# Two attention branches of a decoder trunk: row maxima formed negated, one denominator sum per four blocks, and a new ratio in which the branches are interleaved

## The chip, the cores and the metric

One Trainium2 chip; the kernel runs as one program on one of its cores. The metric is device time in microseconds (us) of one execution. The profile is one execution of the program taken by the hardware profiler; the unprofiled runs are timed on their own.

## What is computed

A decoder layer over 2048 tokens of width 1024: a normalised and modulated input, one wide projection, two attention branches, their merge through gates and an output projection, then a SwiGLU feed-forward part and a last norm. What matters here is the two attention branches and their merge, all in float32:

```python
# branch A: 12 heads in three groups of (window, dilation); per head and 128-query block
logits = where(valid, q.k * Dh**-0.5 - slope * distance, -inf)
lse = logsumexp(logits); out = softmax(logits) @ v
# the three groups of a head slot are merged with weights softmax(lse over the groups)
ya = sum_g alpha_g * out_g @ w_up_a
# branch B: 4 heads, causal, with a forgetting bias
s = q.k * Dh**-0.5 + (F[t] - F[s]);  yb = softmax(where(s_pos <= t_pos, s, -inf)) @ v @ w_up_b
merged = sigmoid(gza) * ya + sigmoid(gzb) * yb
```

## The kernel before, in words

The program goes through stages: modulation and first projection with its gates (to about 880 us in the profile), the two attention branches, the up-projection with the gates (`up`), the output projection with the residual (`p3_block`), and the feed-forward part. Large products are written as Strassen-like products (`t_blocks`) of operands split in a high and a low part (`split`, L106 on ACT and L107 on DVE), and three matmuls stand for one (`mm3`, L100 to L102).

**Branch A** (`head_a`): for each of 12 heads and four groups `u` of four 128-query blocks, `scores` runs two matmuls a block into PSUM tile X (L754, L758), adds the bias and takes the row maximum in one DVE instruction (`tensor_tensor_reduce`, L760; the profile shows a second, short one that reads out the accumulator). When all four blocks are done L763 forms the negative of the four maxima (`nm`), and ACT takes the exponential (L768). `sums` transposes the result on PE (L785), copies it out (L792), multiplies with the values (L796) and lets ACT copy the sum to `utok` (L808). At a head's end its maxima are transposed (L814) and stored in `sta`.

**Branch B** (`head_f`): for each of 4 heads and 16 query blocks (8 pairs `cq`), `scores` goes over 512-key segments: POOL forms the bias `bi` (L838, and L843 on the diagonal), PE the scores (L850), DVE the sum with the running maximum `mx` (L852), then the negative of the last one (L858, `nmf`), ACT the exponentials with their sums `dp` (L862), and DVE adds the segment sums of the block to one denominator (L864). `sums` takes, after every second pair, the reciprocal of four denominators (L869), transposes them (L871) and stores them (`rc`), and for every pair transposes the exponentials (L886), splits them (L106, L107, tiles `ph` and `pl`) and multiplies with the values (L894).

**The merge** (`merge_load`, `merge_weights`): from the stored maxima and denominators of the three groups come the weights `mw`, which go to DRAM as `wrow` (L970). `up` loads the branch outputs `uw` (L981) and the weights spread over the partitions (L987), multiplies and adds them on POOL or DVE (L989, L991), splits them to `y`, and for eight column blocks loads a weight panel (L1001) and gates `gt` (L1008), runs 12 matmuls into PSUM tile Z for each half (L100 to L102, `psZ<-y,wu`), multiplies by the gate on DVE (L1014) and adds on POOL (L1015).

**The order of the work.** `branch_a` and `branch_b` are generators that yield a cost after each step; `together` advances the one whose clock is lower, with A's cost multiplied by `PACE[0]`. A's steps sum to 12 x 4 x 3.5 = 168, B's to 167.2 (per head 136 x 0.175 for the scores and 18 for the sums). A's factor of 0.6 therefore puts its end at 100.8 on B's clock, six tenths of the way through B. After that B goes on alone until it is half way through its last head (`f_done >= 14`), then `up(0)` is interleaved with the rest of it, and `up(1)` follows. A scheduler then moves the instructions of each engine by its own estimate of their times; each engine, and each queue that issues transfers, takes its instructions strictly in the order that comes out. All transfers here are issued by SP's queue. Tiles come from slots with a fixed number of buffers: `wh` and `wl` hold B's exponentials and later gates of `up(1)`, `pc` A's exponentials and later gates of `up(0)`, `bigx` A's `utok` and later `uw`.

```python
    ga, gb = branch_a(), branch_b()
    together([(ga, PACE[0]), (gb, 1.0)])
    merge_weights()
    together([(gb, 1.0)], lambda: f_done[0] >= 4 * (NHB - 1) + 2)
    gu = up(0)
    together([(gu, PACE[1]), (gb, 1.0)])
    for g in (gb, gu, up(1)):
        for _ in g: pass
```

## Time and profile before

| what | value |
|---|---|
| median of three runs | 2900.26 us (2892.75 to 2901.07) |
| the profiled execution's own time | 2897.54 us |
| its span, first to last instruction | 2895.8 us |
| PE, DVE, ACT, POOL busy | 96%, 70%, 48%, 7% of the span |
| mean granted TensorE clock | 0.988 |

PE is TensorE's matmuls, PEld its weight loads, DVE VectorE, ACT ScalarE, POOL GpSimd, SP the engine whose queue issues the transfers. A busy share is that of the whole span; the stages differ, so the rows further down are taken by stretch. A wait is put down to what ended it. [...]

### The profile page before, as it was taken

How to read it: one execution, taken by the hardware profiler on the slowest of the kernel's cores; microseconds unless marked ns; L12 is line 12 of the kernel's file. 1: busy time of each engine (PE TensorE's matmuls, PEld its weight loads, DVE VectorE, ACT ScalarE, POOL GpSimd, SP SyncE). 2: the span in 40 equal slices, each digit the busy share in tenths (PEclk: the TensorE clock that was granted, in tenths of full speed). 3: DMA queues.
4: the chain of work that ended last, by engine and by line, in shares of the span. 5: the costliest groups of instructions: out<-in, count | busy, mean ns of one | idle time of the engine just before them, and what ended most of it. 6: DMA issues, size and time to landing. Idle time of an engine off the chain costs nothing.

```text
span 2895.8 us, 40840 instructions
## 1 busy us (share of the span) xinstructions
PE 2774.1 (96%) x13778; PEld 2309.5 (80%) x13778; DVE 2041.0 (70%) x4269; ACT 1376.4 (48%) x2726; POOL 213.9 (7%) x305
## 2 busy tenths in 40 slices
PE   7999999999999999888899999999999999989998
PEld 6789888978887878666677788888888888868876
DVE  5865578576646887687967766657755558795987
ACT  4654335344447777653356533335333335343543
POOL 0000000000002222563200000000000000000000
PEclk9999999999999999998999999999999999999999
DMA  7687466467757668569766554444522235785642
GB/s 242 166 226 220 131 207 204 148 168 212 235 176 261 239 176 259 144 176 310 265 211 207 189 178 138 135 146 137 164 86 79 83 109 179 217 264 168 219 155 99
DMA packets 520858, 530.52 MB, mean 183 GB/s; under 512 B 91556, under 2 KB 372540, under 8 KB 514236
## 3 DMA queue, kind: packets, MB, share of 16 engines
q1 hardware_dynamic: 520648, 527.91, 58.6%
q8 instruction: 108, 1.77, 0.3%
q14 instruction: 102, 0.84, 0.1%
HBM read 356.51 MB, written 171.29 MB: 182 GB/s over the span
## 4 chain that ended last, share of the span: by engine, by line
PE 47%; DVE 3%; ACT 1%; DMA 1%; issue 1%; DVEq 0%; ACTq 0%
PE psX L100 9%; PE psX L101 9%; PE psX L102 9%; PE psZ L100 4%; PE psZ L101 4%; PE psZ L102 4%; PE psY L101 2%; PE psY L102 2%; PE psY L100 2%; DVE wl L107 0%; DVE wt L217 0%; PE psT L1090 0%; ACT wh L106 0%; ACT u L244 0%; DMA wr<-act 0%
## 5 line engine op out<-in xcount | busy, mean ns | idle before, releaser
L106 ACT ACTIVATE wh<-wt 128x512 fp32r<-128x512 f32 (+1 forms) x464 | 288.5, 623 | 637.0 <-PE psX L101 344.6
L107 DVE TENSOR_TENSOR wl<-wt,wh 128x512 fp32r<-128x512 f32 (+1 forms) x464 | 314.6, 681 | 257.8 <-ACT wh L106 240.6
L106 ACT ACTIVATE wh<-wr 128x512 fp32r<-128x512 f32 (+1 forms) x324 | 201.5, 623 | 433.1 <-PE psX L101 239.1
L107 DVE TENSOR_TENSOR wl<-wr,wh 128x512 fp32r<-128x512 f32 (+1 forms) x324 | 220.0, 680 | 200.9 <-ACT wh L106 183.2
L217 DVE TENSOR_TENSOR wt<-wr 128x512 f32<-128x512 f32 (+1 forms) x216 | 146.5, 678 | 12.0 <-DMA wr<-in_w_in_dram 5.1
L217 DVE TENSOR_TENSOR wt<-wr,wt 128x512 f32<-128x512 f32 (+1 forms) x216 | 147.8, 684 | 3.8
L244 ACT ACTIVATE u<-psX 128x512 f32<-128x512 f32 x216 | 125.3, 580 | 8.1 <-PE psX L102 8.1
L838 POOL TENSOR_SCALAR bi<-nf,F_col 128x512 f32<-128x512 f32 (+3 forms) x160 | 104.9, 658 | 229.3 <-DVE mx L852 192.3
L862 ACT ACTIVATE L<-L,nmf 128x512 f32<-128x512 f32 (+3 forms) x160 | 103.1, 647 | 20.7 <-DVE nmf L858 20.5
L894 PE MATMUL psY<-ph,vhl 128*128 128x256 f32 (+1 forms) x288 | 82.4, 299 | 9.1 <-ACT ph L106 7.8
L1120 DVE TENSOR_TENSOR ac<-psZ,u 128x512 f32<-128x512 f32 x88 | 60.4, 687 | 42.2 <-PE psZ L102 41.2
L894 PE MATMUL psY<-pl,vhl 128*128 128x256 f32 (+1 forms) x288 | 81.8, 312 | 7.8 <-DVE pl L107 6.8
L106 ACT ACTIVATE ph<-psT 128x512 fp32r<-128x512 f32 (+1 forms) x101 | 56.2, 568 | 53.5 <-PE psT L886 53.3
L796 PE MATMUL psY<-pf,va 128*65 128x128 f32 (+1 forms) x408 | 77.7, 324 | 1.3 <-DVE pf L792 0.9
L760 DVE CUSTOM_DVE_ANT_0 L<-psX,bias 128x128 f32<-128x128 f32 (+1 forms) x192 | 64.6, 357 | 19.8 <-PE psX L758 14.1
L107 DVE TENSOR_TENSOR pl<-psT,ph 128x512 fp32r<-128x512 f32 (+1 forms) x101 | 64.5, 646 | 16.2 <-ACT ph L106 16.0
L768 ACT ACTIVATE L<-L,nm 128x128 f32<-128x128 f32 (+1 forms) x192 | 72.1, 450 | 5.5 <-DVE nm L763 4.5
L100 PE MATMUL psZ<-y,wu 128*128 128x512 f32 x128 | 55.7, 435 | 18.7 <-DVE gt L1014 11.5
L100 PE MATMUL psX<-f_A11h,wh 128*128 128x512 f32 x176 | 69.4, 394 | 0.0
L894 PEld LDWEIGHTS psY<-ph,vhl 128*128 128x128 f32 x288 | 56.7, 197 | 15.6 <-ACT ph L106 10.9
L102 PE MATMUL psX<-f_A11h,wl 128*128 128x512 f32 x176 | 69.1, 393 | 0.0
L101 PE MATMUL psX<-f_A11l,wh 128*128 128x512 f32 x176 | 69.1, 392 | 0.0
(536 smaller groups left out, 8732.6 us busy)
## 6 DMA issues: line engine op xcount, KB each, us to landing
x<-x SPq DMA_DIRECT2D x192, 256.0 KB
wr<-in_w_ffn_in_dram SPq DMA_DIRECT2D x88, 512.0 KB
wr<-in_w_in_dram SPq DMA_DIRECT2D x64, 512.0 KB
qk<-sh SPq DMA_DIRECT2D x192, 128.0 KB
act<-ac SPq DMA_DIRECT2D x88, 256.0 KB
pc<-wfg SPq DMA_DIRECT2D x77, 256.0 KB
qk<-st SPq DMA_DIRECT2D x128, 128.0 KB
wa<-in_w_ada_dram SPq DMA_DIRECT2D x64, 256.0 KB
```

The costliest lines, as they stand in the source:

```text
L100: PE.matmul(o, lh, rh, start=first, stop=False, skip_group_check=True)
L101: PE.matmul(o, lh, rl, start=False, stop=False, skip_group_check=True)
L102: PE.matmul(o, ll, rh, start=False, stop=last, skip_group_check=True)
L106: A.activation(hi, src, AF.Copy)
L107: V.tensor_tensor(lo, src, raw(hi), op=ALU.subtract)
L217: V.tensor_tensor(v[i], *made[i](g, v), op=ALU.subtract)
L244: A.activation(t, o, AF.Copy, scale=1.0 if scale is None else scale)
L768: A.activation(Lb(b, o0, 256), Lb(b, o0, 256), AF.Exp, bias=nm[:, bb:bb + 1])
L796: PE.matmul(uo[:65, qb_[0] * P:qb_[0] * P + w], va[:, 4 * u + kb_, :], pf[:, pos:pos + w], start=i_ == 0, stop=i_ == len(runs) - 1, skip_g ...
L838: G.tensor_scalar(bi[:, :e - sg], nf[sg // D][:, sg % D:sg % D + e - sg], 1.0, F_col[:, qb * NHB + h:qb * NHB + h + 1], op0=ALU.mult, op1= ...
L862: A.activation(Ls[cq, b, sg][:, :e - sg], Ls[cq, b, sg][:, :e - sg], AF.Exp, bias=nm, accum_out=dp[:, i:i + 1])
L894: PE.matmul(uo[:, q0:256], vhl[:, kb, :], p_[:, 256 * i:256 * i + 256 - q0], start=(kp == 0 and i == 0 and j == 0), stop=(last and i == 1 ...
```

## The change

A `tensor_tensor_reduce` with scale -1 and a minimum in place of a maximum writes the negated score and accumulates the negated row maximum; the exponential is taken with scale -1. So L763 (48 instructions) and L858 (64) are gone, and A's exponential of a block needs that block's reduction alone. The merge takes a minimum of negated maxima and turns one subtraction round. B's segment sums of four blocks lie in one tile and are added by one instruction just before the reciprocal: 16 in place of 64. `PACE[0]` goes from 0.6 to 0.82, which puts A's end at 168 x 0.82 = 137.8 on B's clock; B's last head is half through at 136.7. A filler tile grows from 16 to 32 columns. In the changed kernel the lines are a few lower: L753 and L755 are A's scores, L765 its exponential, L793 its product with the values, L811 its last transpose, L836 and L841 B's bias, L848 its scores, L857 its exponential, L881 and L889 its transposes and products, L965 `wrow`, L976 and L982 `uw`, L984 and L986 the products of the merge, L996 the panel, L1003 the gates, L1010 POOL's addition.

```diff
-PACE = (0.6, 0.6)
+PACE = (0.82, 0.6)
...
-    cst.tile([P, 16], F32, name="fill")
+    cst.tile([P, 32], F32, name="fill")
     ident = cst.tile([P, P], F32, name="ident")
...
         G.tensor_scalar(bias, base, float(slopes[h] * d), 0.0, op0=ALU.mult, op1=ALU.add)
-        mx = sm.tile([P, NT], F32, tag="mxa", name="mxa")
         nm = sm.tile([P, NT], F32, tag="nm", name="nm")
...
                 V.tensor_tensor_reduce(out=Lb(b, o0, 256), in0=so[:, o0:], in1=bias[:, o0:],
-                                       scale=1.0, scalar=NEG, op0=ALU.add, op1=ALU.max,
-                                       accum_out=mx[:, bb:bb + 1])
-            V.tensor_scalar(nm[:, 4 * u:4 * u + 4], mx[:, 4 * u:4 * u + 4], -1.0, None,
-                            op0=ALU.mult)
+                                       scale=-1.0, scalar=-NEG, op0=ALU.add, op1=ALU.min,
+                                       accum_out=nm[:, bb:bb + 1])
             for b in range(4):
...
                 o0 = P if first[b] else 0
-                A.activation(Lb(b, o0, 256), Lb(b, o0, 256), AF.Exp, bias=nm[:, bb:bb + 1])
+                A.activation(Lb(b, o0, 256), Lb(b, o0, 256), AF.Exp, bias=nm[:, bb:bb + 1], scale=-1.0)
             return Lb, first
...
             pst = ps("Y")
-            PE.transpose(pst[:NT, :P], mx, ident)
+            PE.transpose(pst[:NT, :P], nm, ident)
             str_ = slot("pc", "str", [NT, P])
...
             if cq % 2 == 0 and b == 0:
-                den[cq // 2] = sm.tile([P, 4], F32, tag="den", name="den", bufs=4)
+                den[cq // 2] = [sm.tile([P, 4, cq // 2 + 1], F32, tag=f"dp{cq // 2}", name="dp"),
+                                sm.tile([P, 4], F32, tag="den", name="den")]
             qb = 2 * cq + b
             nk = (qb + 1) * P
-            dq = den[cq // 2][:, qb % 4:qb % 4 + 1]
-            mx = sm.tile([P, 4], F32, tag="mx", name="mx", bufs=4)
+            dp = den[cq // 2][0][:, qb % 4, :]
+            nm = sm.tile([P, 4], F32, tag="nmf", name="nmf", bufs=4)
             segs = list(range(0, nk, CH))
...
                     out=L[:, :e - sg], in0=s[:, :e - sg], in1=bi[:, :e - sg],
-                    scale=1.0, scalar=NEG if i == 0 else mx[:, i - 1:i],
-                    op0=ALU.add, op1=ALU.max, accum_out=mx[:, i:i + 1])
+                    scale=-1.0, scalar=-NEG if i == 0 else nm[:, i - 1:i],
+                    op0=ALU.add, op1=ALU.min, accum_out=nm[:, i:i + 1])
             n = len(segs)
-            nm = sm.tile([P, 1], F32, tag="nmf", name="nmf", bufs=4)
-            V.tensor_scalar(nm, mx[:, n - 1:n], -1.0, None, op0=ALU.mult)
-            dp = sm.tile([P, 4], F32, tag="dp", name="dp", bufs=4)
             for i, sg in enumerate(segs):
                 e = min(sg + CH, nk)
-                A.activation(Ls[cq, b, sg][:, :e - sg], Ls[cq, b, sg][:, :e - sg], AF.Exp, bias=nm,
-                             accum_out=dp[:, i:i + 1])
-            V.tensor_reduce(out=dq, in_=dp[:, :n], op=ALU.add, axis=mybir.AxisListType.X)
+                A.activation(Ls[cq, b, sg][:, :e - sg], Ls[cq, b, sg][:, :e - sg], AF.Exp,
+                             bias=nm[:, n - 1:n], scale=-1.0, accum_out=dp[:, i:i + 1])
...
             if cq % 2:
-                dn = den[cq // 2]
+                dp, dn = den[cq // 2]
+                V.tensor_reduce(out=dn, in_=dp, op=ALU.add, axis=mybir.AxisListType.X)
                 V.reciprocal(dn, dn)
...
         for g in (1, 2):
-            V.tensor_tensor(v3(M, g), v3(M, g), tok(g), op=ALU.max)
+            V.tensor_tensor(v3(M, g), v3(M, g), tok(g), op=ALU.min)
         for g in range(3):
-            V.tensor_tensor(v3(es[g], g), tok(g), v3(M, g), op=ALU.subtract)
+            V.tensor_tensor(v3(es[g], g), v3(M, g), tok(g), op=ALU.subtract)
             A.activation(es[g], es[g], AF.Exp)
```

Three places show what the change does to the order of the instructions. Rows are those of one engine, in its order; a number behind x says how many like it follow each other.

**PE, where branch A ends.** The matmuls of the two branches and of `up` stand between the first score matmul (number 0) and the last of `up` (number 2,813 in both programs). Before, A's last instruction is number 1,815, the first row here, and what follows is B alone (scores L850, transposes L886, products L894):

```order
L814 MATMUL psY<-ident,mxa 16x128
L886 MATMUL psT<-ident,L 128x128 x4
L894 MATMUL psY<-ph,vhl 128x256
L871 MATMUL psY<-ident,den 4x128
L850 MATMUL psX<-kh,qs 128x512
L850 MATMUL psX<-kl,qs 128x512
L894 MATMUL psY<-pl,vhl 128x256
L894 MATMUL psY<-ph,vhl 128x256
L894 MATMUL psY<-pl,vhl 128x256
```

Of the change, numbers 1,826 to 1,837:

```order
L753 MATMUL psX<-kl,qs 128x128
L889 MATMUL psY<-ph,vhl 128x256
L753 MATMUL psX<-kh,qs 128x128
L753 MATMUL psX<-kl,qs 128x128
L753 MATMUL psX<-kh,qs 128x128
L753 MATMUL psX<-kl,qs 128x128
L889 MATMUL psY<-pl,vhl 128x256
L889 MATMUL psY<-ph,vhl 128x256
L889 MATMUL psY<-pl,vhl 128x256
L889 MATMUL psY<-ph,vhl 128x256
L848 MATMUL psZ<-kh,qs 128x512
L848 MATMUL psZ<-kl,qs 128x512
```

A's scores (L753) stand here between B's. A's last instruction is number 2,154, so 339 instructions of B have moved ahead of A's end; the first matmul of `up` is number 2,315 (before 2,158), and B's last one number 2,427 (before 2,547).

**POOL and SP, at the merge.** POOL forms B's bias and, in the same queue, multiplies the branch outputs with the merge weights (`uw`). Before, from the last rows ahead of the first such product on:

```order
L838 TENSOR_SCALAR bi<-nf,F_col 128x512
L843 AFFINE_SELECT bi<-bi 128x128
L989 TENSOR_TENSOR uw<-uw 128x1024
L838 TENSOR_SCALAR bi<-nf,F_col 128x512 x2
L838 TENSOR_SCALAR bi<-nf,F_col 128x384
L989 TENSOR_TENSOR uw<-uw 128x1024
L991 TENSOR_TENSOR uw<-uw 128x1024
L838 TENSOR_SCALAR bi<-nf,F_col 128x512
L843 AFFINE_SELECT bi<-bi 128x128
```

and B's bias goes on like this: 47 bias instructions and 18 diagonals stand behind the first product. Of the change, to the point from which there is no bias any more:

```order
L841 AFFINE_SELECT bi<-bi 128x128
L836 TENSOR_SCALAR bi<-nf,F_col 128x512
L984 TENSOR_TENSOR uw<-uw 128x1024
L836 TENSOR_SCALAR bi<-nf,F_col 128x512
L984 TENSOR_TENSOR uw<-uw 128x1024
L986 TENSOR_TENSOR uw<-uw 128x1024
L836 TENSOR_SCALAR bi<-nf,F_col 128x512 x2
L986 TENSOR_TENSOR uw<-uw 128x1024
L841 AFFINE_SELECT bi<-bi 128x128
L984 TENSOR_TENSOR uw<-uw 128x1024
```

Here three bias instructions and one diagonal are left behind the first product. SP's queue takes gates and panels of `up` ahead of the weights now. Before, the rows up to the weights (`wrow`) are:

```order
L811 DMA u_200<-utok 64x2048
L812 DMA den<-utok 1x2048
L943 DMA md<-sta 32x16x4
L874 DMA rc<-dro 4x128
L936 DMA md<-den 128x64
L981 DMA uw<-u_199 128x1024
L970 DMA wrow<-mw 128x64 x3
L987 DMA uw<-wrow 64x1024 x6
```

and of the change:

```order
L901 DMA u_202<-uy 64x512
L1003 DMA gt<-g_0_163 128x512
L1003 DMA gt<-g_1_132 128x512
L1003 DMA gt<-g_1_164 128x512
L996 DMA wr<-in_w_up_a_dram 128x2x128
L996 DMA wr<-in_w_up_b_dram 128x2x128
L869 DMA rc<-dro 4x128
L1003 DMA gt<-g_0_135 128x512
L1003 DMA gt<-g_0_167 128x512
L965 DMA wrow<-mw 128x64 x3
L1003 DMA gt<-g_1_136 128x512
L982 DMA uw<-wrow 64x1024 x6
```

Four weight panel transfers and seven gate transfers stand ahead of the spread weights (two of the panels and the first gate a few rows further up), where before the first panel stood 27 transfers behind `wrow`.

**ACT, where the exponentials begin.** The last gates of the projection stage take a sigmoid (L445, L448), and going over to an exponential takes a table load. Before:

```order
L862 ACT_TABLE_LOAD
L862 ACTIVATE L,dp<-L,nmf 128x128
L445 ACT_TABLE_LOAD
L445 ACTIVATE st<-psX 128x512
L448 ACTIVATE st<-st 128x512
L768 ACT_TABLE_LOAD
L768 ACTIVATE L<-L,nm 128x128
L768 ACTIVATE L<-L,nm 128x256 x3
L862 ACTIVATE L,dp<-L,nmf 128x256
L862 ACTIVATE L,dp<-L,nmf 128x384
L448 ACT_TABLE_LOAD
```

and of the change:

```order
L765 ACT_TABLE_LOAD
L765 ACTIVATE L<-L,nm 128x128
L448 ACT_TABLE_LOAD
L448 ACTIVATE st<-st 128x512 x2
L765 ACT_TABLE_LOAD
L765 ACTIVATE L<-L,nm 128x256
L244 ACTIVATE u_8666<-psX 128x512
L765 ACTIVATE L<-L,nm 128x256
L857 ACTIVATE L,dp<-L,nmf 128x128
L445 ACT_TABLE_LOAD
L445 ACTIVATE st<-psX 128x512
L765 ACT_TABLE_LOAD
```

A's exponentials go one by one, between the sigmoids, and the table is loaded nine times before it stays, in place of five; in the whole program there are 14 loads in place of 10.

## Rows read from the trace of the kernel before

**Rows 1.** The page's first two parts: the span with busy time, share and instruction count of PE and DVE, and the granted clock in 40 slices (tenths).

```profile
span 2895.8 us, 40840 instructions
...
PE 2774.1 (96%) x13778; PEld 2309.5 (80%) x13778; DVE 2041.0 (70%) x4269; ACT 1376.4 (48%) x2726; POOL 213.9 (7%) x305
...
PEclk9999999999999999998999999999999999999999
```

**Rows 2.** Busy time of the engines by stretch: both branches, B alone, `up`, the gap behind it, and the output projection. Columns: length, then busy us (and instructions) of PE, PEld, DVE, ACT and POOL, the granted clock, the DMA engines' busy share, GB/s.

```profile
880.00:1178.00 298.00, 282.80 (x1994) 244.47 (x1993) 240.69 (x942) 232.16 (x556) 82.36 (x164) 1.00 0.71 223
1178.00:1258.00 80.00, 61.39 (x351) 50.21 (x349) 59.32 (x170) 47.12 (x121) 50.24 (x58) 0.89 0.41 109
1258.00:1423.00 165.00, 143.20 (x674) 113.79 (x674) 134.11 (x230) 63.75 (x134) 73.11 (x58) 0.95 0.93 298
1423.00:1448.00 25.00, 18.33 (x62) 13.18 (x63) 25.00 (x41) 10.82 (x19) 1.58 (x1) 0.80 0.45 141
1448.00:1550.00 102.00, 100.20 (x469) 81.46 (x467) 73.25 (x173) 56.34 (x120) 0.00 (x0) 1.00 0.64 207
```

**Rows 3.** Where the stretches begin and end: A's last transpose and the matmuls of `up`, from the views of line 814 and of tile y (duration min/median/max in ns, first and last start in us).

```profile
L814 PE MATMUL psY<-ident,mxa x12: 271/272/277, 919.5 to 1178.5; 128*16 128x128 f32 x12
```

```profile
L100 PE MATMUL psZ<-y,wu x128: 388/395/797, 1257.8 to 1417.9; 128*128 128x512 f32 x128
L106 ACT ACTIVATE y<-uw x16: 612/626/632, 1212.6 to 1359.7; 128x512 fp32r<-128x512 f32 x16
```

**Rows 4.** PE's waits from 1178 to 1258 us: what waited for what, total us, times, longest.

```profile
PE psY L894 <- ACT ph L106: 5.2, 5, 2.1
PE psY L894 <- DVE pl L107: 3.5, 4, 2.4
PE psX L850 <- DVE mx L852: 3.4, 4, 1.8
PE psZ L850 <- DVE mx L852: 3.1, 3, 1.6
```

**Rows 5.** POOL in order of time behind A's end (start us, us, instruction, and in brackets the idle time before it and what ended it).

```profile
1187.18 0.29 POOL L843 TENSOR_SCALAR_AFFINE_SELECT bi<-bi 128x128 f32<-128x128 f32 x1
1196.70 2.40 POOL L989 TENSOR_TENSOR uw<-uw 128x1024 f32<-128x1024 f32 x1 [9.23 <-issue]
1199.07 2.94 POOL L838 TENSOR_SCALAR bi<-nf,F_col 128x512 f32<-128x512 f32 x3
1201.98 2.37 POOL L989 TENSOR_TENSOR uw<-uw 128x1024 f32<-128x1024 f32 x1
```

**Rows 6.** ACT in order of time in the same stretch, two rows.

```profile
1197.71 0.38 ACT L901 ACTIVATE ulf<-psY 64x256 f32<-64x256 f32 x1 [3.00 <-PE psY L894]
1201.72 0.72 ACT L862 ACTIVATE L<-L,nmf 128x512 f32<-128x512 f32 x1 [3.63 <-DVE nmf L858]
```

**Rows 7.** SP's queue in order of time at the merge (start us, us, line, transfer, count).

```profile
1184.90 0.34 SPq L936 DMA_DIRECT2D md<-den  x1
...
1190.36 1.27 SPq L970 DMA_DIRECT2D wrow<-mw  x3
1191.81 3.66 SPq L987 DMA_DIRECT2D uw<-wrow  x6
```

**Rows 8.** PE's and DVE's waits from 1258 to 1448 us, the longest.

```profile
PE psZ L100 <- DVE gt L1014: 11.5, 10, 4.6
PE psZ L100 <- ACT wu L106: 6.4, 2, 3.5
```

```profile
DVE gt L1014 <- PE psZ L102: 8.3, 10, 2.1
DVE wu L107 <- ACT wu L106: 6.1, 1, 6.1
```

**Rows 9.** Bytes moved from 1178 to 1258 us and from 1258 to 1423 us, one line of each answer of the transfer view.

```profile
DMA packets 4385, 8.76 MB, mean 109 GB/s; under 512 B 1597, under 2 KB 2137, under 8 KB 4313
```

```profile
DMA packets 35880, 49.23 MB, mean 298 GB/s; under 512 B 3006, under 2 KB 17866, under 8 KB 35867
```

**Rows 10.** The instructions that the change removes: groups by line on DVE from 875 to 1450 us (count, busy us and mean ns, idle before and what ended it).

```profile
L864 DVE TENSOR_REDUCE den<-dp 128x1 f32<-128x1 f32 (+3 forms) x64 | 9.4, 148 | 14.8 <-ACT L L862 14.5
...
L858 DVE TENSOR_SCALAR nmf<-mx 128x1 f32<-128x1 f32 x64 | 9.0, 142 | 0.2
...
L763 DVE TENSOR_SCALAR nm<-mxa 128x4 f32<-128x4 f32 x48 | 8.3, 173 | 0.2
```

**Rows 11.** Waits from 880 to 1178 us that hang on them: of ACT, and of DVE.

```profile
ACT L L862 <- DVE nmf L858: 7.9, 9, 2.0
...
ACT L L768 <- DVE nm L763: 4.5, 8, 1.2
```

```profile
DVE den L864 <- ACT L L862: 7.1, 8, 2.7
```

**Rows 12.** Table loads in order of time on ACT, and the busy times of 880 to 900 us (columns as in rows 2).

```profile
891.95 1.28 ACT L448 ACT_TABLE_LOAD   x1 [0.27 <-issue]
893.24 0.63 ACT L448 ACTIVATE st<-st 128x512 f32<-128x512 f32 x1
893.78 0.47 ACT L106 ACTIVATE ph<-psT 128x384 fp32r<-128x384 f32 x1
894.26 1.28 ACT L768 ACT_TABLE_LOAD   x1
895.56 0.91 ACT L768 ACTIVATE L<-L,nm 128x256 f32<-128x256 f32 x2
```

```profile
880.00:900.00 20.00, 17.42 (x97) 13.62 (x95) 9.81 (x45) 17.43 (x34) 4.38 (x9) 1.00 1.03 366
```

## The prediction, made before the changed kernel ran

> **What bounds the kernel now.** I read the page first. PE is busy 96% of the span and DVE 70% [rows 1], so an edit that shortens DVE's work gains only where PE waits. The granted clock shows where to look: it is full except about the middle [rows 1]. The table by stretch then splits the part that the change touches [rows 2]. The reader should see five stretches. With both branches (880 to 1178 us) PE is busy 282.8 of 298 us at full clock: 15.2 us are idle. With B alone (1178 to 1258) it is busy 61.4 of 80 us at a mean clock of 0.89. In the stretch of `up` (1258 to 1423) it is busy 143.2 of 165 at 0.95, while DVE is at 134.1 and the DMA engines at 0.93. In the gap (1423 to 1448) DVE is busy all 25 us and PE waits for it. From 1448 on PE is nearly full. The stretches begin at A's last transpose, 1178.5, and the first matmul of `up`, 1257.8 [rows 3].
>
> The waits tell why B alone is thin. PE waits for B's own chain, the splits and the running maximum [rows 4]. Part of that is a queue: POOL stood 9.2 us before its first product of the merge, with three bias instructions of B right behind it, which ran at 1199 [rows 5]; ACT then waited 3.6 us for a maximum [rows 6]. The product had to wait for the weights, which left for DRAM at 1190.4 and were read back from 1191.8 on [rows 7].
>
> **The change part by part.**
>
> *A's end moves.* Before, A ends at PE instruction 1,815 of the two branches, now at 2,154: 339 of B's instructions are now mixed with A. B alone takes 343 instructions (1,815 to 2,158) in 80 us; its PE work at full clock is 61.4 x 0.89 = 54.6 us [rows 2], or 0.159 us each. The moved 339 are 54 us of work, and at the mixed stretch's busy share (282.8 / 298 = 0.95) 57 us. A ends at 1178.5 + 57 = about 1235. This stretch does not become DVE's: DVE is at 240.7 of 298 there [rows 2].
>
> *The merge has less cover.* From A's end to the first matmul of `up` 161 instructions of B are left, where there were 343. At B's pace alone (80 / 343 = 0.23 us) they take 38 us, at full pace 161 x 0.159 = 26. Beside them runs the merge: before, `md` was loaded 6.4 us behind A's end, `wrow` left after 11.9 us [rows 7], the first split of `y` stood at 34.1 us [rows 3]. POOL has three bias instructions behind the first product now in place of 47, so a stop there keeps little of B back. The bounds are 26 us (merge hidden) and 79 us (all of what lay between before). I take 40 us, nearest to the first `y`: `up` begins at 1275, 17 us later than before.
>
> *`up` gets shorter.* From its first matmul to its last there were 655 PE instructions (2,158 to 2,813) and are now 498; the 157 fewer are B's. B alone kept DVE busy 59.3 us for 343 instructions [rows 2], 0.17 us each, so 27 us of DVE work are gone from here. DVE's work from 1258 to 1448 was 134.1 + 25.0 = 159.1 of 190 us, a share of 0.84 [rows 2]; now 132 us, and at the same share 157 us. I take DVE as what sets the pace, since PE's longest waits there are for the gate product on DVE and for the weight panels [rows 8]. The gap behind `up` then ends at 1275 + 157 = 1432 in place of 1448: **-16 us**. With DVE at a share of 0.95 it would be 139 us and -34; if the transfers set the pace there is no gain (a rival, below).
>
> *The removed DVE instructions.* 48 + 64 + 64 instructions of 8.3, 9.0 and 9.4 us go, and 16 sums (some 2.4 us at 148 ns) come back: 24 us of DVE [rows 10]. DVE is not the bound in the mixed stretch, so this counts only through what waited: ACT 7.9 and 4.5 us for the negated maxima, DVE 7.1 us for the exponentials ahead of the denominator [rows 11]. PE's own idle time there is 15.2 us, and most of what PE waits for hangs on other steps; I take a third, **-5 us** (bounds 0 and -15). A's exponentials now start one by one and not after the fourth block; I count that in the same 5. The sum of denominators is now late by up to four blocks, but nothing waits for it before the gates' weights in `up`.
>
> *More table loads.* ACT loads its table nine times before the exponentials stay, in place of five. A load is 1.28 us, with the next instruction right behind it and 0 to 0.27 us idle before [rows 12]: 4 x 1.28 = 5.1 us. ACT is busy 17.4 of 20 us there [rows 12], so 2.6 us of it have room and **+2.5 us** reach the sigmoids that feed the last gates. The bounds are 0 and +5.1. [...]
>
> The other edits (scale of -1, minimum for maximum, the turned subtraction) leave the number and the shapes of their instructions; I take them as 0, hidden by PE in the mixed stretch.
>
> *Sum.* -16 - 5 + 2.5 = -18.5 us. The profiled execution took 2897.54 us, 2.7 us under the median of the runs, 2900.26. I forecast 2897.5 - 18.5 = **2879 us**. About 0.3%, 8.7 us, is what can be told from no change, so faster means under 2891.6 and slower over 2909.0.
>
> **The rivals.**
>
> *The transfers set the pace of `up`.* Between A's end and the end of `up` 8.76 + 49.23 = 58.0 MB moved [rows 9], and most of it (merged rows, gates, the results) can't move before A is done and its slots are free. At the 298 GB/s of the stretch of `up` [rows 9] that takes 195 us: 1235 + 195 = 1430, and the gap of 25 us ends at 1455, 7 us later than before. With -5 and +2.5 the kernel takes some 2902 us: no change. For it speaks the share of 0.93 in that stretch; against it that B alone left the DMA engines at 0.41 [rows 2], and that eleven gate and panel transfers now stand ahead of the weights in SP's queue, so the waits for panels [rows 8] can go.
>
> *The merge is laid bare (slower).* The eleven transfers in front of the spread weights wait for slots that B's and A's last transposes free, and SP's queue is strict. If the weights are late and the first matmul of `up` comes 80 us behind A's end as before, it stands at 1315; with 157 us from there the gap ends at 1472, +24, and the kernel takes 2897.5 + 24 - 2.5 = 2919 us. PE would have 26 us of work for those 80. It decides from a first `up` matmul at 1275 + 18.5 + 8.7 = 1302 on. Against it: before, the first `y` was there 34 us behind A's end, and the panel's place in the queue held the rest back.
>
> *More than forecast.* If DVE reaches 0.95 in `up`, since POOL's stops no longer hold B back, the gain there is 34 us and the time 2897.5 - 34 - 2.5 = 2861 us.
>
> That the change does not do what it says I rule out: the orders show A's end and the counts of instructions as told.
>
> **How the numbers follow.** The forecast, a gain of 9 to 28 us, gets 0.50; more than that 0.18; the transfers 0.22; the bare merge 0.10. So faster by over 0.3% is 0.68, no change 0.22, slower 0.10. The range leaves out the bare merge and the tail beyond the larger gain: 2855 (some 6 us beyond the larger gain) to 2905 (just above the transfers' 2902). The likeliest case alone lies between 2870 and 2889.
>
> **What would show it.** Right: A's last transpose near 1235, the first `up` matmul near 1275, full clock up to A's end, PE near full again from about 1432, L763 and L858 gone with their waits, nine table loads of 1.28 us. Wrong: a busy share of the mixed stretch under 0.93 (B cannot keep up on one score tile); a first `up` matmul after 1302; or a stretch of `up` as long as before with the DMA engines over 0.93, which would be the transfers.

## The result and the profile after

The changed kernel takes **2933.1 us** (median of 4 runs, 2931.5 to 2934.8), the kernel before 2899.5 beside it: a ratio of 1.012 (95% interval 1.0103 to 1.0138). It is slower by 1.2%, where 2879 us and a gain were forecast; it lies outside the range. The profiled execution took 2934.34 us.

The stretches of [rows 2], cut at the same events in the profile after (length; busy us and count of PE, PEld, DVE, ACT, POOL; granted clock; DMA share; GB/s):

```profile
880.00:1243.00 363.00, 338.25 (x2339) 291.78 (x2338) 274.43 (x942) 278.82 (x667) 107.86 (x213) 0.98 0.59 185
1243.00:1283.00 40.00, 30.38 (x164) 23.10 (x164) 27.97 (x77) 25.90 (x68) 24.51 (x27) 0.91 0.62 163
1283.00:1453.00 170.00, 122.16 (x498) 93.31 (x497) 109.13 (x157) 40.73 (x74) 67.50 (x41) 0.90 0.95 294
1453.00:1485.00 32.00, 25.02 (x90) 17.94 (x89) 31.10 (x50) 14.01 (x27) 2.54 (x2) 0.84 0.49 154
1485.00:1587.00 102.00, 100.18 (x469) 81.45 (x468) 72.95 (x171) 55.83 (x119) 0.00 (x0) 1.00 0.61 202
```

The third row is the surprise. `up` holds 498 PE instructions in place of 674 and DVE is busy 109 us in place of 134, and yet it is longer: 170 us in place of 165. The last stretch is as before, so everything was lost ahead of it: it begins at 1485 in place of 1448. The events themselves, which answer to [rows 3] (ns min/median/max, first and last start):

```profile
L811 PE MATMUL psY<-ident,nm x12: 270/273/274, 930.1 to 1243.3; 128*16 128x128 f32 x12
```

```profile
L100 PE MATMUL psZ<-y,wu x128: 387/394/796, 1282.8 to 1452.8; 128*128 128x512 f32 x128
...
L107 DVE TENSOR_TENSOR y<-uw,y x16: 676/689/1828, 1282.5 to 1378.7; 128x512 fp32r<-128x512 f32 x16
```

A ends at 1243.3 (forecast 1235) and the first `up` matmul stands 39.5 us behind it (forecast 40). Inside `up`, two windows of 20 us show a hole:

```profile
1320.00:1340.00 20.00, 7.62 (x24) 5.63 (x24) 8.39 (x11) 1.78 (x3) 6.38 (x5) 0.74 0.95 292
1340.00:1360.00 20.00, 8.83 (x25) 6.53 (x26) 9.43 (x11) 2.30 (x4) 8.03 (x5) 0.78 1.04 311
```

In neither of them is a compute engine busy for half of the time; the DMA engines are full. The waits name what is late: PE's from 1243 to 1485, and ACT's from 1283 to 1400 (total us, times, longest), against [rows 8]:

```profile
PE psZ L100 <- ACT wu L106: 24.2, 4, 10.8
PE psZ L100 <- DVE gt L1009: 11.7, 11, 1.9
```

```profile
ACT wu L106 <- DMA wr<-in_w_up_b_dram: 46.1, 9, 15.5
ACT y L106 <- DVE uw L986: 15.2, 2, 14.8
```

PE waits for a panel, and ACT, which splits it, for the panel's transfer and for the merged rows. The transfer view of 1283 to 1380 us, the stretch of the 16 merged rows, has:

```profile
DMA packets 14027, 27.89 MB, mean 288 GB/s; under 512 B 1605, under 2 KB 4169, under 8 KB 14022
...
q1 hardware_dynamic: 14022, 27.83, 98.2%
```

So the 16 DMA engines are full from the first row to the last. Whether that sets the length of `up` is another question, which e3 answers below.

### The profile page after: what moved, and what is told of

It is laid out like the page before. It is cut to its first block, busy times and chain, and to the rows that moved or that the text cites. A ratio compares the mean times of both kernels' runs of the same rounds, so it can differ in the third digit from the quotient of the medians.

```text
span 2932.6 us, 40726 instructions
## 1 busy us (share of the span) xinstructions
PE 2783.6 (95%) x13778; PEld 2313.7 (79%) x13778; DVE 2022.4 (69%) x4109; ACT 1382.2 (47%) x2730; POOL 209.1 (7%) x305
## 4 chain that ended last, share of the span: by engine, by line
PE 81%; DMA 7%; DVE 6%; ACT 4%; issue 2%; SPq 1%; POOL 0%; DVEq 0%; ACTq 0%; POOLq 0%
PE psX L100 13%; PE psX L101 13%; PE psX L102 13%; PE psZ L100 7%; PE psZ L102 7%; PE psZ L101 7%; PE psY L100 3%; PE psY L101 3%; PE psY L102 3%; PE psY L793 2%; PE psY L889 2%; PE psZ L848 1%; DMA gt<-g 1%; DMA uw<-wrow 1%; PE psT L782 1%
## 5 line engine op out<-in xcount | busy, mean ns | idle before, releaser
L107 DVE TENSOR_TENSOR wl<-wt,wh 128x512 fp32r<-128x512 f32 (+1 forms) x464 | 314.9, 682 | 259.0 <-ACT wh L106 243.7
L107 DVE TENSOR_TENSOR wl<-wr,wh 128x512 fp32r<-128x512 f32 (+1 forms) x324 | 219.8, 679 | 197.3 <-ACT wh L106 183.4
L836 POOL TENSOR_SCALAR bi<-nf,F_col 128x512 f32<-128x512 f32 (+3 forms) x160 | 102.8, 645 | 267.7 <-DVE nmf L850 241.7
L857 ACT ACTIVATE L<-L,nmf 128x512 f32<-128x512 f32 (+3 forms) x160 | 103.3, 648 | 29.6 <-DVE nmf L850 29.1
L889 PE MATMUL psY<-pl,vhl 128*128 128x256 f32 (+1 forms) x288 | 82.7, 315 | 10.3 <-DVE pl L107 9.7
L765 ACT ACTIVATE L<-L,nm 128x128 f32<-128x128 f32 (+1 forms) x192 | 78.1, 456 | 19.5 <-DVE nm L759 18.8
L889 PE MATMUL psY<-ph,vhl 128*128 128x256 f32 (+1 forms) x288 | 82.8, 300 | 1.8 <-ACT ph L106 1.5
L107 DVE TENSOR_TENSOR pl<-psT,ph 128x512 fp32r<-128x512 f32 (+1 forms) x101 | 64.9, 652 | 21.8 <-ACT ph L106 21.6
L793 PE MATMUL psY<-pf,va 128*65 128x128 f32 (+1 forms) x408 | 77.6, 323 | 2.3 <-DVE pf L789 2.1
L889 PEld LDWEIGHTS psY<-pl,vhl 128*128 128x128 f32 x288 | 57.1, 198 | 18.7 <-DVE pl L107 16.8
L100 PE MATMUL psZ<-f_S4h,wh 128*128 128x512 f32 x176 | 68.7, 390 | 0.2 <-DVE ac L1115 0.2
```

Source lines behind the costliest of these rows:

```text
L100: PE.matmul(o, lh, rh, start=first, stop=False, skip_group_check=True)
L107: V.tensor_tensor(lo, src, raw(hi), op=ALU.subtract)
L765: A.activation(Lb(b, o0, 256), Lb(b, o0, 256), AF.Exp, bias=nm[:, bb:bb + 1], scale=-1.0)
L793: PE.matmul(uo[:65, qb_[0] * P:qb_[0] * P + w], va[:, 4 * u + kb_, :], pf[:, pos:pos + w], start=i_ == 0, stop=i_ == len(runs) - 1, skip_g ...
L836: G.tensor_scalar(bi[:, :e - sg], nf[sg // D][:, sg % D:sg % D + e - sg], 1.0, F_col[:, qb * NHB + h:qb * NHB + h + 1], op0=ALU.mult, op1= ...
L857: A.activation(Ls[cq, b, sg][:, :e - sg], Ls[cq, b, sg][:, :e - sg], AF.Exp, bias=nm[:, n - 1:n], scale=-1.0, accum_out=dp[:, i:i + 1])
```

## The experiments

Each run is shown by four times (us, from its profiled execution): A's end, the first `up` matmul, the last split of `y` (all merged rows in) and the last `up` matmul. The length is that of `up`, from its first matmul to its last. Most of the difference lies there: behind the last `up` matmul another 1475 to 1487 us follow in every run but e3 (1491) and e4 (1493). Ratios are to the kernel before, with 95% intervals.

| run | A's end | first up | last y | last up | length | median us | ratio |
|---|---|---|---|---|---|---|---|
| before | 1178.5 | 1257.8 | 1360.5 | 1417.9 | 160 | 2899.5 | |
| after | 1243.3 | 1282.8 | 1378.7 | 1452.8 | 170 | 2933.1 | 1.012 (1.0103-1.0138) |
| e1 | 1251.8 | 1290.2 | 1377.5 | 1446.4 | 156 | 2931.7 | 1.0117 (1.0102-1.0132) |
| e2 | 1174.4 | 1249.3 | 1346.3 | 1408.4 | 159 | 2886.8 | 0.9952 (0.9935-0.9969) |
| e8 | 1194.3 | 1244.7 | 1343.5 | 1404.3 | 160 | 2888.4 | 0.9959 (0.9945-0.9973) |
| e11 | 1213.0 | 1258.1 | 1357.9 | 1432.2 | 174 | 2914.7 | 1.006 (1.0045-1.0076) |
| e3 | 1246.4 | 1285.4 | 1380.0 | 1452.4 | 167 | 2945.5 | 1.0164 (1.0147-1.018) |
| e4 | 1181.3 | 1260.6 | 1355.5 | 1424.6 | 164 | 2918.1 | 1.0066 (1.0051-1.0081) |
| e5 | 1245.4 | 1286.1 | 1424.7 | 1483.1 | 197 | 2959.4 | 1.0199 (1.0179-1.022) |
| e6 | 1245.3 | 1286.7 | 1391.0 | 1464.6 | 178 | 2938.2 | 1.0132 (1.0108-1.0157) |
| e7 | 1172.9 | 1246.3 | 1350.7 | 1405.2 | 159 | 2885.2 | 0.9953 (0.9932-0.9973) |
| e10 | 1243.6 | 1283.2 | 1378.2 | 1449.6 | 166 | 2931.5 | 1.0122 (1.0107-1.0137) |
| e13 | 1242.3 | 1282.8 | 1371.1 | 1456.5 | 174 | 2931.9 | 1.0121 (1.0106-1.0136) |
| e14 | 1175.1 | 1249.4 | 1351.0 | 1410.0 | 161 | 2889.6 | 0.9968 (0.9959-0.9978) |
| e15 | 1243.4 | 1283.9 | 1372.2 | 1449.6 | 166 | 2931.8 | 1.0123 (1.0106-1.0139) |
| e9 | 1247.4 | 1287.0 | 1355.4 | 1438.6 | 152 | 2920.8 | 1.0079 (1.0063-1.0096) |
| e12 | 1169.7 | 1244.0 | 1343.2 | 1400.0 | 156 | 2882.0 | 0.9949 (0.9934-0.9964) |
| e16 | 1243.8 | 1284.2 | 1354.7 | 1433.7 | 150 | 2915.0 | 1.0057 (1.0042-1.0072) |
| e17 | 1240.4 | 1280.8 | 1368.0 | 1436.6 | 156 | 2920.8 | 1.009 (1.007-1.011) |
| e18 | 1251.9 | 1261.2 | 1348.2 | 1426.5 | 165 | 2903.8 | 1.0022 (1.0011-1.0033) |

### Which part of the change costs: PACE alone, edits alone, values between

e1 is the kernel before with the new PACE; e2, e8 and e11 are the changed kernel with others.

```diff
-PACE = (0.6, 0.6)      # e1, in the kernel before
+PACE = (0.82, 0.6)
-PACE = (0.82, 0.6)     # in the changed kernel
+PACE = (0.6, 0.6)      # e2; 0.7 in e8, 0.76 in e11
```

> The kernel before with only the ratio changed (0.6 to 0.82). Theory T (after branch A's end some 56 MB have to move at about 295 GB/s, and they set the pace of the up stretch, so that a later end of A is a later end of everything) and theory Q (SP's strict queue puts the loads of the second half of up and of x ahead of the panels of the first half) both expect nearly the whole loss here: 2925 to 2940 us. Theory E (the edits to the maxima, the denominators and the four more table loads cost the time) expects 2895 to 2905.

> The changed kernel with the ratio put back to 0.6, so that only the negated maxima and the summed denominators are left. T and Q expect within 6 us of the kernel before, 2893 to 2905 (some microseconds won by 24 us less of DVE work, some lost to table loads). E expects 2925 to 2940.

> The edits with a ratio of 0.7: A ends at PE instruction 1,966 (0.6: 1,815; 0.82: 2,154), and the first matmul of up stays at 2,162 as with 0.6 (2,156). If the loss comes only once B left behind A's end is too short to cover the merge's 40 us (196 instructions are some 46 us at B's pace alone), this is as fast as 0.6 or up to 8 us faster: 2878 to 2888. If each microsecond of a later end of A costs, it is 10 us or more slower: over 2897.

> The changed kernel with the first PACE at 0.76 in place of 0.82; A's last transpose stands at PE number 2,071 (1,966 at 0.70, 2,154 at 0.82). Theory S (up starts some 40 us behind A's end once less than that is left of B, takes its own 160 us, and what is moved ahead of A's end is lost in full): A's end near 1218, the first up matmul near 1258 to 1262, 8 to 13 us later than at 0.60, and the kernel 2896 to 2902. Rival: the loss sits only in the hole of the 0.82 order (a queue order that this one need not have): then 2887, as at 0.60 and 0.70. Third: the loss goes with the moved instructions one for one (46 us for 339): 256 of 339, 2922.

The new PACE alone costs the whole loss (e1), and the edits alone gain 0.5%, 14 us (e2): this is the version that beats both. With the edits, going from 0.60 to 0.82 costs 46 us, and the step to 0.70 nothing. A's end moves on with PACE, but up to 0.70 the B that is left still covers the merge and `up` starts no later (1249, 1245). At 0.76 the start is 1258 as expected, 45 us behind A's end, but `up` takes 174 us, so 28 us are lost and not 9 to 15. The column of the length is the point: `up` takes 159 us with some 655 PE instructions up to its last matmul (e2) and 156 with 465 (e1); in the change it takes 170 with 498. So fewer instructions of B beside `up` did not make it shorter: those that stood there were free. The stretches of e2, and `up` in e1:

```profile
880.00:1174.00 294.00, 281.12 (x1993) 245.06 (x1992) 229.88 (x815) 233.95 (x557) 82.19 (x164) 0.99 0.73 226
1174.00:1249.00 75.00, 61.80 (x345) 50.89 (x344) 56.11 (x145) 48.30 (x121) 50.01 (x57) 0.82 0.45 120
1249.00:1409.00 160.00, 138.00 (x660) 109.34 (x660) 131.80 (x213) 63.37 (x131) 75.09 (x60) 0.97 0.93 300
```

```profile
1290.00:1447.00 157.00, 120.81 (x469) 89.25 (x469) 110.68 (x144) 36.53 (x63) 69.12 (x41) 0.89 0.98 313
```

In the stretch of `up` PE did 138.0 us of work in e2 and 122.2 after the change, and e2 took less time for it.

### Fewer gate bytes

```diff
-                    for i in range(2):
-                        SP.dma_start(gts[i], g_scr[8 * i + j][2 * cp + c_])
+                    SP.dma_start(gts[0], g_scr[j][2 * cp + c_])
...
-                    V.tensor_tensor(gt, o, gt, op=ALU.mult)
+                    V.tensor_tensor(gts[1 - i], o, gts[0], op=ALU.mult)
```

> The changed kernel without the loads of branch B's gates in up (the other gate is used twice): 32 loads of 256 KB, 8.4 MB, are left out, all instructions of the engines stay. T expects the up stretch shorter by 8.4 MB / 294 GB/s = 28 us: about 2905. Q expects the panels to stay behind other loads and 5 to 10 us less: 2923 to 2928.

> The kernel before with the same 8.4 MB left out. T expects that up was paced by the transfers there too: some 25 us less, 2870 to 2880. The view of the prediction, that DVE paced up, expects under 6 us less: 2893 to 2900. Q, for which only the changed kernel's queue is at fault, expects under 10.

8.4 MB fewer, and `up` is 3 us shorter in the one kernel and 4 longer in the other. Both programs are slower, and they lose most of it behind `up`. The merged rows come no earlier (e3, the last split of `y` at 1380.0). So not every byte weighs, and `up` is nearly as long with DMA engines that aren't full: in e3 they were busy for 76% of the time from A's end to the last `up` matmul (second view; 88% in the change), and half idle just where the rows were done (third):

```profile
L107 DVE TENSOR_TENSOR y<-uw,y x16: 669/688/1765, 1286.0 to 1380.0; 128x512 fp32r<-128x512 f32 x16
```

```profile
DMA packets 33153, 47.80 MB, mean 231 GB/s; under 512 B 3981, under 2 KB 17317, under 8 KB 33075
...
q1 hardware_dynamic: 33140, 47.65, 76.1%
```

```profile
1360.00:1380.00 20.00, 17.49 (x66) 11.98 (x65) 10.85 (x17) 2.55 (x5) 7.18 (x5) 0.96 0.51 158
```

What ends last in e3 isn't settled. From 1283 to 1400 us SP's queue stood 30.1 us for the sums of POOL that it stores, against 4.8 us in the change, so this edit may have put one wait in the place of another.

### The order in the queues

Four tries at the order: e5 holds all loads of the second half, and the residual's `x`, behind the first half's last panel; e6 issues the stores `m` from ACT's queue, e7 does the same with the edits alone (PACE 0.60), and e10 issues the panels from ACT's queue, where they no longer wait for one of B's stores either.

```diff
+                with tc.issue_after(panel[1]) if cp else ExitStack():     # e5: uw, its weights, gates, x
                     SP.dma_start(uu, ...)
...
-                SP.dma_start(m_scr[2 * cp + c_][j], gts[0])               # e6, e7
+                A.dma_start(m_scr[2 * cp + c_][j], gts[0])
...
-                    SP.dma_start(r[:, 2 * i:2 * i + 2, :], ...)           # e10
+                    A.dma_start(r[:, 2 * i:2 * i + 2, :], ...)
```

> The changed kernel (2933) with one thing moved: the loads of the second half of up (merged rows, weights, gates) and the first loads of x stand behind the last panel of the first half in SP's queue. Theory Q1 (those loads, ahead of the panels in the strict queue, make the hole of 40 us from 1320 on) expects the stretch of up to go from 170 to 145 to 158 us: 2908 to 2922. Theory Q2 (the stores of the results, which wait for POOL at the head of the same queue, hold back the panels) and theory L (the stretch has a length of its own, about 160 us, whatever stands beside it) expect 2925 to 2935.

> The changed kernel with the 32 stores of up's results issued from ACT's queue in place of SP's. Q2 expects the 14.5 us that the store waited for POOL in SP's queue back, and more if panels follow it: 2912 to 2920. Q1 expects 2928 to 2935, L the same.

> The changed kernel with the weight panels of up issued from ACT's queue in place of SP's. Rival O: ACT stands 46 us for panels between 1283 and 1400, nine times, since a panel's issue stands in SP's queue behind waiting stores and loads; from a queue of their own they land in time, the hole at 1320 to 1360 closes and the kernel gains the 11 us by which up is longer than before, 2922 or less. Theory D: the panels are late because the DMA engines are full there, and another queue changes nothing: within 4 us of 2933. A loss is possible too, since ACT issues a panel only behind its own copies.

None of them gains. e5 moved the hole behind the first half and made it longer (197 us), since the second half's rows were then late; e6 is slower than the change or equal to it; e10 is equal (last up 3 us earlier, the interval that of the change). For e7 a gain of 10 to 18 us over e2 was expected if the stores in SP's queue hold the panels back; it is equal to e2. So none of these places in SP's queue is what sets the length.

### The merged rows: fewer of them, and ahead of what isn't needed yet

e9 (in the changed kernel) and e12 (with the edits alone) cut the second half's rows. e13 leaves nothing out: it issues the second half's gates and `x` only behind its last spread weight. e14 does the same with the edits alone, and e15 holds back only `x` in the changed kernel.

```diff
-                SP.dma_start(uu, u_scr[...][:, cs])                       # e9, e12
+                if not cp or not g:
+                    SP.dma_start(uu, u_scr[...][:, cs])
...
-                for i in range(2):
+                for i in range(0 if cp else 2):
                     SP.dma_start(wb[64 * i:64 * i + 64, :], ...)
...
-                with tc.issue_after(hold):                                # e13, and x the same
+                with tc.issue_after(rows[0] if cp else hold):
                     for i in range(2):
                         SP.dma_start(gts[i], ...)
```

> The changed kernel, but the second half of up reads only 4 of its 8 merged rows and none of their spread weights (the row of the first group stands for the others and for the weights, so the merge of the second half is not the reference's); all products and additions stay, 6 MB of about 50 are not loaded, all of them from the middle of up. Theory D (the transfers fill the middle of up: in 1300 to 1360 the DMA share is 0.95 to 1.04 at 270 to 311 GB/s while PE is busy under 9 of 20 us, and the second half's rows are what fills it): 6 MB at 300 GB/s are 20 us, so up takes some 150 us in place of 170 and the kernel 2915. Rival O (the order in SP's queue and the slots set the length of up, whatever the bytes, as with the halved gates): up stays at 165 to 170 and the kernel within 6 us of 2933.

> The same 6 MB left out of the second half of up, with the edits alone (PACE 0.60). Theory D: the middle of up is full of transfers here too (0.97 to 1.00 at 323 GB/s from 1320 to 1360), so up shortens from 159 us, but B's work stands beside it and takes the place: 2875 to 2882. Rival O: nothing changes, 2885 to 2889.

> The changed kernel with the second half's gates and the residual's x loads issued only behind the second half's last spread weights; nothing is left out. Theory D (the second half's rows are late because other transfers share the DMA engines with them; 5.5 MB that are not needed yet go ahead of them): the last y comes 10 to 18 us earlier than 1378.7, the last up matmul near 1437, and the kernel takes 2914 to 2922. Rival C (16 rows through 3 slots take their 97 us whatever is beside them): last y within 4 us of 1378 and the kernel within 6 us of 2933. A loss is possible if the gates are then late for the second half's products.

e9 shortens `up` well below its 170 us: 152 us, near the 150 expected, and last `y` 23 us earlier. The time falls by 12 us, less than 18, with A's end 4 us later in this execution. In e12 `up` is 156 in place of 159 and the ratio that of e2: at a PACE of 0.60 the second half's rows are not what ends last. In e13 the rows come 8 us earlier, but then the second half's gates are late, which POOL shows from 1360 to 1400 us (nothing is gained):

```profile
POOL gt L1010 <- DMA gt<-g: 17.1, 4, 5.9
POOL gt L1010 <- DVE gt L1009: 12.6, 3, 5.9
```

In e15 the last split of `y` comes 6.5 us earlier and the kernel is the change's (2931.8, where 2925 to 2929 were expected if the rows' delay counts). e14 is 3 us slower than e2, with overlapping intervals. So transfers beside the rows do delay the rows, by 6.5 to 8 us, but the theory that bytes not needed yet could go later for nothing fell.

### Which bytes are dear

The trace after has two short stretches with one kind of load nearly alone. Spread weights from 1266 to 1273 us, branch rows from 1233.6 to 1235.2:

```profile
DMA packets 575, 1.64 MB, mean 235 GB/s; under 512 B 110, under 2 KB 110, under 8 KB 575
...
q1 hardware_dynamic: 575, 1.64, 98.8%
```

```profile
DMA packets 189, 0.65 MB, mean 406 GB/s; under 512 B 22, under 2 KB 22, under 8 KB 189
...
q1 hardware_dynamic: 189, 0.65, 100.6%
```

Both times the engines are full, and the spread weights move at 0.58 of the speed. So e16 leaves out the one and e17 the other in the second half, e18 the spread weights of both halves:

```diff
-                for i in range(2):
+                for i in range(0 if cp else 2):                           # e16; range(0) in e18
                     SP.dma_start(wb[64 * i:64 * i + 64, :], ...)
...
-                SP.dma_start(uu, ...)                                     # e17
+                if not cp:
+                    SP.dma_start(uu, ...)
```

> The changed kernel without the loads of the spread weights in the second half of up (4.2 MB; the row is multiplied by itself, so the second half's merge is not the reference's). Theory W (the spread weights are the dear bytes, 235 GB/s with the DMA engines full): 4.2 MB / 235 = 18 us less, last y 1361, up 152 us, the kernel 2915 to 2920. Rival E (each byte weighs alike, 288 GB/s from 1283 to 1380): 14.6 us, 2919 to 2922. Rival C (the slots): nothing.

> The changed kernel without the loads of the branch rows in the second half of up (also 4.2 MB, in 8 transfers in place of 16; the spread weights are multiplied by themselves). Theory W (406 GB/s): 10 us less, last y 1368, up 160 us, the kernel 2922 to 2926. Rival E: 14.6 us, as in the run before. Rival C: nothing.

> The changed kernel without any spread weights (8.4 MB), so that up waits neither for them nor for the merge: up's first matmul stands 40 PE instructions behind A's end. Theory (the whole loss of the changed kernel is A's end, then the merge, then the transfers): 36 us of transfers and up to 35 us of merge go, and the kernel falls to or below the edits alone, 2875 to 2890. If it stays above 2900, moving B ahead of A's end costs something else too.

For the same 4.2 MB the last split of `y` comes 24 us earlier without the spread weights and 11 without the rows (the lines of L107 in e16, then e17; 1378.7 in the change):

```profile
L107 DVE TENSOR_TENSOR y<-uw,y x16: 678/686/1765, 1283.9 to 1354.7; 128x512 fp32r<-128x512 f32 x16
```

```profile
L107 DVE TENSOR_TENSOR y<-uw,y x16: 675/690/2383, 1280.5 to 1368.0; 128x512 fp32r<-128x512 f32 x16
```

The kernels follow: 18 us below the change (18 expected) and 12 (10 expected; equal bytes would give 14.6 for both). The ratios' intervals just touch, so the order of the two rests on the `y` lines more than on the times; e17's 2921 even lies in the range given for equal bytes (2919 to 2922) and not in that for dear ones (2922 to 2926). A rival is left untested: in each slot the spread weights are issued behind the row, and the products of the merge waited for them (in the change ten waits of 21.7 us in all on `uw<-wrow`, none on a row). So leaving them out also takes away what lands last, whatever a byte costs.

e18 missed: 2904 us, not 2875 to 2890. Without the wait for the merge `up` starts 9 us behind A's end, and 29 of the 46 us between e2 and the change come back. Most of that is the earlier start (21.6 us before the change's). But by the expectation's own sign, a time above 2900, moving B ahead of A's end costs something else too. The other 17 are the 12 us by which `up` still starts later than in e2 and its 165 us. Here DVE is the full engine, since B's rest stands beside the start of `up`:

```profile
1260.00:1280.00 20.00, 13.56 (x61) 11.45 (x62) 19.02 (x38) 10.89 (x28) 14.94 (x15) 0.74 0.55 170
1280.00:1300.00 20.00, 18.25 (x104) 14.87 (x104) 19.83 (x40) 12.80 (x30) 15.23 (x13) 1.00 0.56 174
```

## Why the prediction was wrong

**The step that failed is "`up` gets shorter", and in it the choice of DVE as what sets the pace.** It gave -16 us, from 157 us for `up` and the gap. Measured from the first `up` matmul to the end of the gap it was 1282.8 to 1485, 202 us, at a DVE share of (109.1 + 31.1) / 202 = 0.69 and not 0.84. Of the 27 us of DVE work 19 did go away (159.1 to 140.2), and `up` with its gap grew by 12 us: with 190 PE instructions fewer beside it, `up` took 156 us in e1 and 160 in the kernel before. What ends late in the change are the merged rows: without the second half's spread weights or its rows `up` takes 150 or 156 us in place of 170 (e16, e17). The rows stand there at 98% of the DMA engines; that the full engines are the reason is not shown, since in e3 `up` takes 167 us at 76%. In the kernel before the engines were nearly as full (from 1258 to 1360 us 28.3 MB at 277 GB/s and a share of 0.90, after 27.9 MB in 97 us), but that the rows set the pace there too isn't shown, and e12 speaks against it. The sign that the prediction gave for the transfers, a stretch of `up` as long as before with the DMA engines over 0.93, did come (170 us, 0.95). I read the share of 0.93 in [rows 2] as a rival and gave it 0.22; the longest PE waits [rows 8] named DVE, but a wait shows who came last, and their 11.5 us of 190 were too few to carry a gain of 16.

**The rival "the transfers set the pace" came nearest, but its sum is not the mechanism either.** It put the last `up` matmul 195 us behind A's end, from 58.0 MB at 298 GB/s. Measured are 209.5 us: 56.6 MB at 269 GB/s, since from A's end to the first `up` matmul only 163 GB/s moved. Those 14.5 us, A's end 8 us later and a gap of 32 in place of 25 make 30 of the 31 us between its 2902 and the result. e1 would have met its 195 us (194.6). But by the same sum 8.4 MB fewer are 28 us less, and e3 showed 3 us and e4 none.

**A's end, 1235 forecast, 1243.3 measured.** The mixed stretch kept a share of 338.3 / 363 = 0.93 where I took 0.95. e1, which has the table loads of before, kept 342.9 / 372 = 0.92, so the lower share comes with the new mix. Part of it is at its head: PE at 14.7 of 20 us in place of 17.4 [rows 12] (16.6 in e1, and 17.0 in e2 with the same nine table loads), and from 900 to 920 a granted clock of 0.91:

```profile
880.00:900.00 20.00, 14.70 (x80) 11.61 (x79) 7.94 (x33) 18.75 (x31) 4.08 (x8) 1.00 1.05 371
900.00:920.00 20.00, 19.48 (x125) 16.52 (x124) 17.65 (x64) 16.83 (x45) 9.47 (x18) 0.91 0.44 169
```

The rest of the 8 us isn't settled.

**The merge, 40 us, held** (39.5; 9 us without the spread weights, in e18), and with it the detail of POOL: its first product waited 2.1 us for the weights in place of 9.2 [rows 5].

```profile
1268.96 2.35 POOL L984 TENSOR_TENSOR uw<-uw 128x1024 f32<-128x1024 f32 x1 [2.10 <-DMA uw<-wrow]
```

With the gates and panels ahead of the weights in SP's queue the first `up` matmul stood at 1282.8, so the rival of the bare merge, which needed 1302, did not come. But I had the account of the merge wrong: of the 69 us by which A ends later than at 0.60 (e2), the shorter way from A's end to `up` gives 35 back, and the other 33.5 us of later start are lost in full, since `up` gives nothing. That is the loss of this change, with 11 us more for `up`.

**The edits, -2.5 forecast, -14 measured alone** (e2, interval -19 to -9). The removed instructions and their waits are gone as told; the sums of denominators are now 16:

```profile
L863 DVE TENSOR_REDUCE den<-dp 128x4 f32<-128x4 f32 (+3 forms) x16 | 2.5, 158 | 8.1 <-ACT L L857 8.1
```

With 112 + 64 - 16 = 160 instructions fewer, A ends 4 us earlier in e2 and `up` starts 8.5 and ends 9.5 us earlier: the thin stretch of B alone gains as much (4.4 us) as the mixed one (4.1), which I had not counted. What the four more table loads cost within this wasn't measured alone. Behind the new PACE the same edits gain nothing (e1 and the change are equal): there A ends 8.5 us earlier in the change, and `up` takes 14 us longer; why is not shown.

**The table loads** are nine, as told, each 1.28 us:

```profile
889.49 1.28 ACT L448 ACT_TABLE_LOAD   x1
890.79 0.63 ACT L448 ACTIVATE st<-st 128x512 f32<-128x512 f32 x1
891.44 1.28 ACT L765 ACT_TABLE_LOAD   x1
```

The sigmoid stands 0.02 us behind its load.

**What stays open**: why `up` needs 150 to 165 us even with half its spread weights or all of them left out (e16, e18), why 8.4 MB fewer gates leave it as long as it was (e3, e4), and why it took 174 us at 0.76. DVE is full in e18, the second half's gates are late in e13, the rows in the change: I take it that they lie so close to each other that each cut hands the end to the next, but no run shows this as a whole.

## What to carry to other kernels

Before work is moved out of a stretch, show what ends last in that stretch: here an engine with a share of 0.84 beside DMA engines at 0.93 was not it, and the work that stood beside it was free there. A full share of the DMA engines is no proof either: leave a load out and see whether the stretch shrinks (8.4 MB of gates: 3 us; 6.3 MB of rows and weights: 18 us). Work moved ahead of a step that starts a long chain delays the chain, so give it only as much as still covers the chain's fixed head (here 40 to 50 us). Test a schedule number apart from the edits that come with it: here the edits gained 0.5% and the number lost 1.6%.

## What the runs showed of the hardware

The bytes of a transfer are not alike at a full share of the DMA engines: 406 GB/s for rows of 4 KB to 128 partitions (in 1.6 us), 362 for gates, stores and loads of the output projection (1400 to 1440 us, share 1.02), 235 where mostly spread weights move, each transfer one row of 4 KB over 64 partitions. The rates don't add up to a price for each kind: in e13, from 1300 to 1316 us, rows and spread weights together moved at 206 GB/s with the engines full (100.1%), less than either alone. Why the spread weights move at 235 GB/s is not shown: no run separates the 64 partitions of such a transfer from the cost of reading one row 64 times, and one transfer to all 128 partitions was not tried.
